# Weight-part tiles 64 bytes longer, so that the four slots of a ring start at four different offsets modulo 256 bytes

## The chip, the core and the metric

The kernel runs on one core of a Trainium2 chip. The metric is the device time of one execution in microseconds (us). TensorE (PE) multiplies, and its weight loads are listed apart as PEld; VectorE (DVE), ScalarE (ACT), GpSimd (POOL) and SyncE (SP) are the other engines. SBUF is the on-chip memory with 128 partitions; an address below is the byte within one partition, the same for all 128.

## The reference

One layer of a decoder with four parallel branches over 256 tokens of width 2048, all in float32. What matters here is that nearly all of it is products with large weight matrices, each read once:

```
xn = rms_norm(x, ln_g)
cols = jnp.split(w_in, _split_points(), axis=1)
(a_q, a_k, a_v, a_g, c_b, c_c, c_h, c_g, s_q, s_k, s_v, s_g, m_q, m_g,
 i_q, i_k, i_w, r_a, r_c, r_s, r_m) = [xn @ w for w in cols]
...
mk, mv = jnp.split(mem_n @ w_mem_kv, 2, axis=-1)
...
merged = (sigmoid(r_a) * (y_a @ w_branch[0]) + sigmoid(r_c) * (y_c @ w_branch[1])
          + sigmoid(r_s) * (y_s @ w_branch[2]) + sigmoid(r_m) * (y_m @ w_branch[3]))
return x + merged @ w_out
```

A final RMSNorm follows. The four branches are two masked attentions, an attention over 256 memory tokens and a short convolution; each is small beside the products.

## The kernel before, in words

Each float32 operand is split into a high part of type fp32r and the remainder, also fp32r, and a product is three matmuls that add into one PSUM bank: high by high, high by low, low by high. The tokens are split once and stay in SBUF: `x_hl` holds 16 chunks of 128 rows, each 256 high and 256 low values (the memory tokens lie in `m16a` and `m16b`, the gated branch results in `y`, the merged result in `mt`, all in the same form).

The weights stream. `split_weights` (L117) loads 128 partitions x 2048 values at a time on SP's queue into one of four `raw` tiles (L123), and cuts each into two halves of 1024 values. For each half `parts_tiles` (L113) takes the next slot of two rings with four slots each, `hi` and `lo`; `split` (L106) lets ACT write the high part (L107) and DVE the remainder (L108). TensorE then reads the slot. ACT can begin a slot again only when TensorE has finished with it.

There are two shapes of matmul. In `project_t` (L145, matmuls L141 to L143 in `products_t`) the weights are the stationary operand, 128 columns of 4 bytes loaded by PEld, and 256 tokens stream past; one slot serves 24 matmuls. In `project` (L166) and in `by_halves` (matmuls L162 to L164 in `products`) 128 token columns are stationary and 512 weight values stream past, except in the last two blocks of the output projection, where 256 do; one slot serves 12 matmuls in `project`. TensorE executes matmuls in the order of the program, and loads the weights of the next one beside the running one.

Addresses follow from the order and sizes of the tiles. A constant pool with a filler tile ends at byte 24,576, where `x_hl` begins, and then come `qt`, `m16b`, `m16a`, `kt` (8704 bytes, the size of its largest tenant `u`, L612), `vv`, `y`, `nat`, the four `raw`, the four `hi`, the four `lo` (4096 bytes a slot), `part`, `pt`, and a pool with `sm`, `st`, `pr` and `yt`. All sizes up to `sm` are multiples of 256 bytes, so every token tile, every slot and every `raw` tile begins at 0 modulo 256. Each row of a slot that a matmul or a weight load reads is a multiple of 512 bytes into it. Two `st` tiles take 32 bytes each, so the `pr` and `yt` tiles begin at 64 modulo 256. The last tile ends at byte 228,928 of 229,376.

Of the kernel before, what the change touches and what calls it, by code (L numbers as in the profile page):

```python
# [9 lines left out]
F32 = mybir.dt.float32  # L10
F32R = mybir.dt.float32r
# [4 lines left out]
P = 128  # L16
T = 256
# [3 lines left out]
NB = 512  # L21
# [27 lines left out]
def hybrid_kernel(ctx, tc, x, xT, mem, memT, ln_g, mem_ln_g, w_t, w_n, w_idx, conv_w, conv_b, w_mem_k, w_mem_v,  # L49
# [5 lines left out]
    big = ctx.enter_context(tc.tile_pool(name="big", bufs=1))  # L55
    rawp = ctx.enter_context(tc.tile_pool(name="rawp", bufs=4))
    spl = ctx.enter_context(tc.tile_pool(name="spl", bufs=4))
# [53 lines left out]
        return rawp.tile([P, 4 * NB], F32, name="raw", tag="raw").rearrange("p (k c) -> p k c", c=c)  # L111

    def parts_tiles(w=NB, c=NB):  # L113
        return [spl.tile([P, 2 * NB], F32R, name=n, tag=n).rearrange("p (k c) -> p k c", c=w)[:, :, :c]
                for n in ("hi", "lo")]

    def split_weights(src, w):  # L117

        c = src.shape[2]
        per, half = 4 * NB // w, 2 * NB // w  # L120
        for k0 in range(0, src.shape[1], per):
            raw = raw_tile(w)[:, :, :c]
            nc.sync.dma_start(out=raw, in_=src[:, k0:k0 + per])  # L123
            for h0 in range(0, per, half):
                hi, lo = parts_tiles(w, c)
                split(hi, lo, raw[:, h0:h0 + half])
                for k in range(half):
                    yield hi[:, k], lo[:, k], k0 + h0 + k
# [59 lines left out]
    def quarter_parts(raw):  # L188
        for h in (0, 2):
            hi, lo = parts_tiles()  # L190
            split(hi, lo, raw[:, h:h + 2])
            for i in range(2):
                yield hi[:, i], lo[:, i], h + i
# [131 lines left out]
    def to_heads(name, c0):  # L325

        dst = big.tile([P, 8, T], F32, name=name, tag=name)
        for b in range(4):
            copy_t(dst[:, 2 * b:2 * b + 2], project_t(w_t[FIRST[c0] + b], x_act))
        return dst  # L330
# [176 lines left out]
    def first_columns(dst):  # L507

        src = w_t[FIRST[M_Q]:FIRST[M_Q] + 2].rearrange("b p k c -> p k b c")
        outs = [bank("first", tag)[:, :T] for tag in "aabb"]  # L510
        xraw = big.tile([P, KC, T], F32, name="xraw", tag="m16b")
        for k0 in range(0, KC, 4):
            raw = raw_tile(NB).rearrange("p k (b c) -> p k b c", b=2)
            n = 1 if k0 == 0 else 2
            for k in range(k0, k0 + 4, n):
                nc.sync.dma_start(out=xraw[:, k:k + n], in_=xT[:, k:k + n])
                for i in range(n):
                    nc.sync.dma_start(out=raw[:, k + i - k0], in_=src[:, k + i])
                for i in range(n):
                    if (k + i) % 2 == 0:  # L520
                        hi, lo = parts_tiles(NB, NB)
                    split_tokens(xraw[:, k + i], k + i, g_x, x_hl[:, k + i])
                    h, lw = hi[:, (k + i) % 2], lo[:, (k + i) % 2]
                    split(h, lw, raw[:, k + i - k0].rearrange("p b c -> p (b c)"))
                    for j in range(4):
                        js = slice(j * P, (j + 1) * P)
                        products_t(outs[j], h[:, js], lw[:, js], k + i, KC, x_act)
        copy_t(dst[:, 0:4], outs)
# [40 lines left out]
    k = big.tile([P, 8, T], F32, name="kt", tag="kt")  # L569
# [28 lines left out]
    k = to_heads("kt", S_K)  # L598
# [6 lines left out]
    k = to_heads("kt", A_K)  # L605
# [3 lines left out]


    cc = to_heads("qt", C_C)
    u = big.tile([P, 8 * (T + 16)], F32, name="u", tag="kt")[:, :8 * (T + 2)].rearrange("p (c t) -> p c t", c=8)  # L612
    nc.gpsimd.memset(u[:, :, 0:2], 0.0)
    for b in range(4):
        acc = project_t(w_t[FIRST[C_H] + b], x_act)
# [101 lines left out]
```

## Time and profile before

| | |
|---|---|
| runs | 1414.96, 1413.65, 1413.29 us; median 1413.65 |
| profiled execution | 1414.42 us, of which the span from the first to the last instruction is 1412.6 us |
| TensorE granted clock, mean | 0.997 of full speed |
| PE busy | 1396.2 us, 99% of the span |
| PEld busy | 1263.7 us, 89% |
| DVE, ACT busy | 933.8 us (66%), 729.2 us (52%) |
| HBM | 190 GB/s over the span |

A matmul's duration counts from its start to the modelled end of its pipeline, so matmuls overlap in the records and a busy share of 99% does not say that the array runs at its peak. The distance between the starts of two successive matmuls is the time that one costs.

### The profile page before, as it was taken

The numbers are of one execution on the slowest core, as the hardware profiler recorded it, in microseconds if no ns is written. First come the engines' busy times: TensorE is split into PE (matmuls) and PEld (weight loads), VectorE is DVE, ScalarE is ACT, GpSimd is POOL, SyncE is SP. The second block draws the span as 40 slices with busy tenths as digits, with TensorE's granted clock in tenths as the row PEclk, the third lists the DMA queues.
The fourth block names the chain that finished last, engine by engine and source line by source line (L and its number), as shares of the span: only waits on it lengthen the run. The fifth ranks groups of instructions, "written<-read, shape, count | busy, mean of one in ns | idle before, by whom it ended". The sixth has DMA issues, their size and how long they took to land.

```text
span 1412.6 us, 21263 instructions
## 1 busy us (share of the span) xinstructions
PE 1396.2 (99%) x8796; PEld 1263.7 (89%) x8796; DVE 933.8 (66%) x1123; ACT 729.2 (52%) x991; POOL 11.2 (1%) x26
## 2 busy tenths in 40 slices
PE   9999999999999999999999999999999999999997
PEld 9998998789999898877999899878999999878887
DVE  7587764774747885487546876487546557788654
ACT  7663675453445585445444685445433345545443
POOL 1000000000000000000000000000000000000000
PEclk9999999999999999999999999999999999999999
DMA  9764645375553735537554645637555654736561
GB/s 342 285 243 175 208 151 179 120 268 171 178 180 120 268 125 185 198 119 254 193 180 149 238 149 185 203 120 255 193 179 180 212 182 148 267 139 244 180 202 66
DMA packets 49969, 269.49 MB, mean 191 GB/s; under 512 B 6656, under 2 KB 17456, under 8 KB 19024
## 3 DMA queue, kind: packets, MB, share of 16 engines
q1 hardware_dynamic: 48960, 264.03, 54.3%
q0 software_dynamic: 624, 3.31, 0.6%
q8 instruction: 69, 1.13, 0.3%
q10 hardware_dynamic: 288, 0.79, 0.1%
q14 instruction: 28, 0.23, 0.0%
HBM read 265.88 MB, written 2.10 MB: 190 GB/s over the span
## 4 chain that ended last, share of the span: by engine, by line
PE 87%; DVE 7%; DMA 2%; issue 2%; ACT 2%; SPq 0%; POOLq 0%; POOL 0%; DVEq 0%; ACTq 0%
PE acc L141 14%; PE acc L143 14%; PE acc L142 14%; DVE lo L108 4%; PE w L163 4%; PE w L164 4%; PE w L162 4%; PE r L162 3%; PE r L163 3%; PE r L164 3%; PE o L162 2%; PE o L163 2%; PE o L164 2%; DMA raw<-in_w_n 1%; PE y L163 1%
## 5 line engine op out<-in xcount | busy, mean ns | idle before, releaser
L108 DVE TENSOR_TENSOR lo<-raw,hi 128x1024 fp32r<-128x1024 f32 (+1 forms) x538 | 639.5, 1201 | 432.0 <-ACT hi L107 430.4
L107 ACT CAST hi<-raw 128x1024 fp32r<-128x1024 f32 (+1 forms) x538 | 551.7, 1032 | 559.1 <-PE acc L142 212.1
L142 PE MATMUL acc<-x_hl,hi 128*128 128x256 f32 x1520 | 431.2, 284 | 0.0
L143 PE MATMUL acc<-x_hl,lo 128*128 128x256 f32 x1520 | 431.0, 284 | 0.0
L141 PE MATMUL acc<-x_hl,hi 128*128 128x256 f32 x1520 | 430.5, 283 | 0.0
L142 PEld LDWEIGHTS acc<-x_hl,hi 128*128 128x128 f32 x1520 | 290.8, 191 | 0.2
L141 PEld LDWEIGHTS acc<-x_hl,hi 128*128 128x128 f32 x1520 | 290.7, 191 | 0.2
L143 PEld LDWEIGHTS acc<-x_hl,lo 128*128 128x128 f32 x1520 | 290.6, 191 | 0.1
L162 PE MATMUL w<-hi,y 128*128 128x512 f32 x256 | 99.9, 390 | 0.0
L164 PE MATMUL w<-hi,y 128*128 128x512 f32 x256 | 99.6, 389 | 0.0
L163 PE MATMUL w<-lo,y 128*128 128x512 f32 x256 | 99.6, 389 | 0.0
L162 PE MATMUL r<-hi,x_hl 128*128 128x512 f32 x248 | 96.9, 391 | 0.0
L163 PE MATMUL r<-lo,x_hl 128*128 128x512 f32 x248 | 96.6, 389 | 0.0
L164 PE MATMUL r<-hi,x_hl 128*128 128x512 f32 x248 | 96.5, 389 | 0.0
L164 PEld LDWEIGHTS w<-hi,y 128*128 128x128 f32 x256 | 48.1, 188 | 10.0
L162 PEld LDWEIGHTS w<-hi,y 128*128 128x128 f32 x256 | 48.1, 188 | 9.9
L163 PEld LDWEIGHTS w<-lo,y 128*128 128x128 f32 x256 | 48.1, 188 | 9.8
L162 PE MATMUL o<-hi,mt 128*128 128x512 f32 (+1 forms) x160 | 55.4, 347 | 0.0
L163 PE MATMUL o<-lo,mt 128*128 128x512 f32 (+1 forms) x160 | 55.3, 347 | 0.0
L162 PEld LDWEIGHTS r<-hi,x_hl 128*128 128x128 f32 x248 | 46.7, 188 | 9.6
L164 PE MATMUL o<-hi,mt 128*128 128x512 f32 (+1 forms) x160 | 55.3, 347 | 0.0
L164 PEld LDWEIGHTS r<-hi,x_hl 128*128 128x128 f32 x248 | 46.6, 188 | 9.6
(247 smaller groups left out, 1858.1 us busy)
## 6 DMA issues: line engine op xcount, KB each, us to landing
raw<-in_w_t SPq DMA_DIRECT2D x92, 1024.0 KB, 5.0
raw<-in_w_n SPq DMA_DIRECT2D x80, 1024.0 KB, 4.9
raw<-in_w_branch SPq DMA_DIRECT2D x32, 1024.0 KB, 5.2
raw<-in_w_out SPq DMA_DIRECT2D x16, 1024.0 KB, 4.8
raw<-in_w_mem_k SPq DMA_DIRECT2D x8, 1024.0 KB, 5.6
raw<-in_w_mem_v SPq DMA_DIRECT2D x8, 1024.0 KB, 5.1
raw<-in_w_t SPq DMA_DIRECT2D x16, 256.0 KB, 5.7
raw<-in_memT SPq DMA_DIRECT2D x2, 1024.0 KB, 8.0
```

What stands on the lines that cost most here:

```text
L107: nc.scalar.copy(out=hi, in_=src)
L108: nc.vector.tensor_sub(out=lo, in0=src, in1=hi.bitcast(F32))
L141: nc.tensor.matmul(o, lhsT=hi, rhs=a[:, 0], start=(k == 0), stop=False)
L142: nc.tensor.matmul(o, lhsT=hi, rhs=a[:, 1], start=False, stop=False)
L143: nc.tensor.matmul(o, lhsT=lo, rhs=a[:, 0], start=False, stop=(k == nk - 1))
L162: nc.tensor.matmul(o, lhsT=ah, rhs=hi, start=start, stop=False)
L163: nc.tensor.matmul(o, lhsT=ah, rhs=lo, start=False, stop=False)
L164: nc.tensor.matmul(o, lhsT=al, rhs=hi, start=False, stop=stop)
```

## The change

Each `hi` and `lo` tile is allocated 16 values (64 bytes) longer, and the matmuls, casts and subtractions use the first 1024 values as before. Slots of a ring now lie 4160 bytes apart, so slots 0 to 3 start at 0, 64, 128 and 192 modulo 256. A ring takes 16,640 bytes, 65 times 256, so the `lo` ring starts at 0 again and `hi` and `lo` of the same slot share their offset. To make room `u` is allocated with 8 x 264 instead of 8 x 272 values (8448 bytes, 33 times 256): the tiles from `vv` to the `hi` ring move down by 256 bytes, and those behind the `lo` ring up by 256. Their offsets modulo 256 stay. No instruction is added, removed or reshaped.

```
     def parts_tiles(w=NB, c=NB):
-        return [spl.tile([P, 2 * NB], F32R, name=n, tag=n).rearrange("p (k c) -> p k c", c=w)[:, :, :c]
+        return [spl.tile([P, 2 * NB + 16], F32R, name=n, tag=n)[:, :2 * NB].rearrange("p (k c) -> p k c", c=w)[:, :, :c]
                 for n in ("hi", "lo")]
...
-    u = big.tile([P, 8 * (T + 16)], F32, name="u", tag="kt")[:, :8 * (T + 2)].rearrange("p (c t) -> p c t", c=8)
+    u = big.tile([P, 8 * (T + 8)], F32, name="u", tag="kt")[:, :8 * (T + 2)].rearrange("p (c t) -> p c t", c=8)
```

## Rows read from the trace of the kernel before

**Rows 1.** The page: busy time of each engine (us, share of the span, instructions), TensorE's granted clock in 40 slices in tenths, and the chain that ended last, by engine and by line.

```profile
PE 1396.2 (99%) x8796; PEld 1263.7 (89%) x8796; DVE 933.8 (66%) x1123; ACT 729.2 (52%) x991; POOL 11.2 (1%) x26
...
PEclk9999999999999999999999999999999999999999
...
PE 87%; DVE 7%; DMA 2%; issue 2%; ACT 2%; SPq 0%; POOLq 0%; POOL 0%; DVEq 0%; ACTq 0%
PE acc L141 14%; PE acc L143 14%; PE acc L142 14%; DVE lo L108 4%; PE w L163 4%; PE w L164 4%; PE w L162 4%; PE r L162 3%; PE r L163 3%; PE r L164 3%; PE o L162 2%; PE o L163 2%; PE o L164 2%; DMA raw<-in_w_n 1%; PE y L163 1%
```

**Rows 2.** The whole span as one window, busy time with counts in brackets: instructions that read or write a `hi` tile, then those of a `lo` tile, then the matmuls of L141 and those of L162 alone. The last row is the group of 256-value matmuls of L162 from the groups kept apart by shape.

```profile
0.00:1412.60 1412.60, 1286.77 (x5608) 940.93 (x5608) 639.49 (x538) 551.71 (x538) 1.00 0.55 191
...
0.00:1412.60 1412.60, 903.23 (x2804) 531.69 (x2804) 639.49 (x538) 1.00 0.55 191
...
0.00:1412.60 1412.60, 482.98 (x1712) 1.00 0.55 191
...
0.00:1412.60 1412.60, 411.01 (x1092) 1.00 0.55 191
...
L162 PE MATMUL o<-hi,mt 128*128 128x256 f32 x64 | 17.9, 283 | 0.0
```

**Rows 3.** The timeline of PE from 700 to 706 us, 256 streamed columns: start in us, duration in us, instruction. First and last of 53 matmuls.

```profile
699.73 0.28 PE L142 MATMUL acc<-x_hl,hi 128*128 128x256 f32 x1
...
705.97 0.28 PE L143 MATMUL acc<-x_hl,lo 128*128 128x256 f32 x1
```

**Rows 4.** The timeline of PE from 560 to 563 us, 512 streamed columns. First and last of 15 matmuls.

```profile
559.71 0.39 PE L164 MATMUL r<-hi,x_hl 128*128 128x512 f32 x1
...
562.89 0.39 PE L163 MATMUL r<-lo,x_hl 128*128 128x512 f32 x1
```

**Rows 5.** The timeline of PE from 98.9 to 103 us, 512 streamed columns, just after a change of shape. The 0.48 us of the first matmul has a wait in it.

```profile
98.72 0.48 PE L162 MATMUL v<-hi,m16a 128*128 128x512 f32 x1
99.03 0.40 PE L163 MATMUL v<-lo,m16a 128*128 128x512 f32 x1
99.27 0.40 PE L164 MATMUL v<-hi,m16a 128*128 128x512 f32 x1
99.50 0.40 PE L162 MATMUL v<-hi,m16a 128*128 128x512 f32 x1
99.74 0.39 PE L163 MATMUL v<-lo,m16a 128*128 128x512 f32 x1
...
101.12 0.39 PE L163 MATMUL v<-lo,m16a 128*128 128x512 f32 x1
101.35 0.39 PE L164 MATMUL v<-hi,m16a 128*128 128x512 f32 x1
```

**Rows 6.** The timeline of PE from 343 to 345 us, where 68 weight columns are stationary instead of 128 and 256 tokens stream. First and last of 17 such matmuls.

```profile
343.07 0.28 PE L141 MATMUL acc<-x_hl,hi 128*68 128x256 f32 x1
...
344.94 0.28 PE L142 MATMUL acc<-x_hl,hi 128*68 128x256 f32 x1
```

**Rows 7.** Groups kept apart by shape: weight loads with 256 columns streaming beside them, and with 512 (busy us, mean ns of one, idle us before).

```profile
L141 PEld LDWEIGHTS acc<-x_hl,hi 128*128 128x128 f32 x1504 | 288.5, 192 | 0.2
...
L162 PEld LDWEIGHTS w<-hi,y 128*128 128x128 f32 x256 | 48.1, 188 | 9.9
```

**Rows 8.** The timeline of PE at 491 us and at 355 us: two passes of a plain float32 matmul, once with the streamed operand `pr` at 64 and the stationary `vv` at 0 modulo 256, once with both operands in `it` at 0.

```profile
491.91 0.39 PE L394 MATMUL yp<-pr,vv 128*128 128x128 f32 x2
...
355.45 0.39 PE L458 MATMUL lg<-it 128*128 128x128 f32 x2
```

**Rows 9.** Groups kept apart by shape on DVE and ACT: 512 values with both inputs at 0, then twice with one input at 64 and one at 0, and the cast to `y` or `hi` from 64 and from 0.

```profile
L502 DVE TENSOR_TENSOR merged<-merged,sig 128x512 f32<-128x512 f32 x24 | 15.6, 682 | 0.0
...
L344 DVE TENSOR_TENSOR yt<-yt,qt 128x512 f32<-128x512 f32 x16 | 11.0, 686 | 2.1 <-ACT qt L429 2.0
L108 DVE TENSOR_TENSOR y<-yt,y 128x512 fp32r<-128x512 f32 x16 | 10.9, 684 | 0.7 <-ACT y L107 0.7
...
L107 ACT CAST y<-yt 128x512 fp32r<-128x512 f32 x16 | 9.9, 616 | 1.5 <-DVE yt L344 1.5
...
L107 ACT CAST hi<-raw 128x512 fp32r<-128x512 f32 x16 | 9.4, 615 | 3.7 <-DMA raw<-in_w_t 3.6
```

**Rows 10.** The splits of full halves, by shape, and the waits of ACT before them (who waited for whom: us in total, times, longest).

```profile
L108 DVE TENSOR_TENSOR lo<-raw,hi 128x1024 fp32r<-128x1024 f32 x518 | 626.9, 1222 | 418.4 <-ACT hi L107 416.9
L107 ACT CAST hi<-raw 128x1024 fp32r<-128x1024 f32 x518 | 540.6, 1050 | 548.8 <-PE acc L142 205.5 <-PE w L164 95.1 <-PE r L164 71.3
...
ACT hi L107 <- PE acc L142: 212.1, 128, 2.5
...
PEld m L163 <- DVE lo L108: 5.0, 5, 1.1
```

## The prediction

> **What bounds the kernel now.** I read the page first: PE is busy for 99% of the span, the chain that ended last lies on PE for 87% and on DVE for 7%, and TensorE's granted clock is at its upper level, 2.4 GHz, in every slice [rows 1]. So the time is the number of matmuls times the distance between their starts, plus a few stretches where PE waits for a split. Next come the counts: 5608 matmuls read a `hi` tile and 2804 a `lo` tile, 8412 of 8796 together. L141 has 1712 of them, L162 has 1092 [rows 2]; each stands for three lines of equal count, so 5136 belong to `project_t` and 3276 to the other shape. Of the latter 3 x 64 = 192 stream 256 values, which makes 5328 matmuls that stream 256 columns and 3084 that stream 512.
>
> Then the distances. From 699.73 to 705.97 us there are 52 steps, 6.24 / 52 = 0.120 us each [rows 3]. From 559.71 to 562.89 there are 14 steps, 3.18 / 14 = 0.227 us [rows 4]. At 2.4 GHz 256 columns last 106.7 ns and 512 last 213.3 ns. Each matmul thus costs about 13.3 ns more than its columns, whichever shape it has. That surplus, 8412 x 13.3 ns = 112 us, is the only thing that the change can reach on TensorE. The question is whether it has to do with where the stationary and the streamed operand lie relative to each other.
>
> **What the trace says of that.** Before, every weight slot and every token tile starts at 0 modulo 256, so no row shows a weight part at another offset. Three views come near.
>
> First, the surplus isn't a constant. Just after a change of shape, the same 512-column matmul goes from 99.03 to 99.74 us in three steps, 0.237 us each, and from 99.03 to 101.35 in ten, 0.232 [rows 5]; later it settles at 0.227. With 68 stationary columns in place of 128 the 256-column matmul goes from 343.07 to 344.94 in 16 steps, 0.117 [rows 6]. And a weight load lasts 192 ns beside 256 streaming columns, 188 beside 512 [rows 7]. So the load and the stream do act on each other, and how much depends on their timing. The Trainium skill (SBUF — State Buffer, "Who interferes with whom") gives TensorE two independent read ports and says "PE and ACT never wait on anyone"; by it the change moves nothing at all, 0 us. These rows agree with it only in part: something in the pair of streams moves by up to 10 ns at one and the same offset.
>
> Second, the one matmul in which the operands differ by 64: two passes of `yp` with `pr` at 64 against `vv` at 0 take 0.39 us, and two passes of `lg` with both at 0 take 0.39 us as well [rows 8]. The distance of 64 costs nothing that shows. But this is plain float32, 128 columns at a time; it streams fewer values per ns than fp32r, so it is near evidence and no proof.
>
> Third, the other engines: a subtraction or product with one input at 64 and one at 0 takes 684 to 686 ns where both at 0 take 682, and a cast takes 616 from 64 and 615 from 0 [rows 9].
>
> **The change part by part.**
> - Longer tiles, on TensorE: three of four slots move to a new offset, so 3/4 of the matmuls are touched: 3996 of 256 columns and 2313 of 512, 6309 in all. Price unknown, bounded from both sides. From below, the whole surplus of these goes: 6309 x 13.3 ns = -84 us. From above, the surplus stays at the worst distance of the disturbed stretch, 0.237 instead of 0.227, for the 512-column shape, 2313 x 10 ns = +23 us, and, taking the same 10 ns for the other shape, 3996 x 10 = +40 us, together +63 us. The nearest row is that of the two float32 matmuls, 0.39 against 0.39, so I take 0. A step of 10 ns in two durations of two passes each leaves up to 5 ns a pass unseen there, which is why both other signs keep their chances.
> - Longer tiles, on DVE and ACT: 518 full splits of 1222 ns and 1050 ns [rows 10]. DVE's subtraction then reads `hi` at one offset and `raw` at another. By the row with unequal inputs this is +4 of 682 ns, 0.6%: 7 ns a split, 518 x 7 = 3.7 us of DVE time. It is hidden: ACT starts a split only when TensorE has freed a slot, and waits for this 212.1 us in the 256-column stages alone [rows 10]. Where it isn't hidden, DVE's 4% of the chain for L108, some 57 us, 0.6% is 0.3 us. I take 0; without the cover the whole 3.7 us would show.
> - `u` shorter, and tiles moved by 256 bytes: no offset modulo 256 changes, no instruction is reshaped, each convolution row keeps its place inside `u`. 0 us.
> - DMA: `raw` keeps its offset, sizes and order. 0 us. No wait is added, and the ring still has four slots.
>
> Sum: 1412.6 + 0 for the span. The profiled execution took 1414.42 us, 1.8 more than its span; the median of the runs is 1413.65, 0.8 below it. My forecast is the median, **1413.7 us**.
>
> **Rivals.** What a measurement of this kernel can tell from no change is about 0.2%, 2.8 us. Over 6309 matmuls that is 0.45 ns each, so if the offset matters to the surplus at all, the result will hardly look like no change.
>
> Slower: the load and the stream start within a few ns of each other, and at equal offsets they fall into the 0.227 that the 512-column shape settles at, which is the low end of what it shows. If the offset decides where they meet, slots at 64, 128 and 192 settle higher, or each new slot starts a stretch as after 99.03 us. At 0.232 this is 2313 x 5 ns = +12 us, 1425; with the whole 10 ns on this shape +23 us, 1437. It decides from 2.8 us / 2313 = 1.2 ns on. For it: the disturbed stretch, which is slower at every one of its first steps, and that a slot serves only 12 matmuls in `project`. Against: the two equal float32 pairs.
>
> Faster: the 256-column shape settles at 0.120, above the 0.117 of the 68-column loads. If equal offsets are what makes the two streams meet, the other three slots come down to 0.117, 3996 x 3 ns = -12 us, and if the 512-column shape gains as much, 2313 x 3 = -7 us: 1395. For it: the shorter load leaves the same stream faster, so part of the surplus is the load's. Against: half the columns save only 3 of 13 ns, and a load of half the length isn't another offset. The Trainium skill (TensorE: Matmul & The Clock Gate, "Back-to-back issue gap") puts the isolated warm gap at the columns over 2.4 GHz plus about 2.5 ns; by that estimate 10.8 ns of the surplus could go, 6309 x 10.8 = -68 us, 1346. No row here of an fp32r matmul comes near that gap.
>
> That the change doesn't do what it says: if the pool rounded sizes up to 256 bytes, all slots would stay at 0. The `pr` tile's 64, which two 32-byte `st` tiles make, speaks against it. It would also give 1413.7 and is part of the first case.
>
> **How the numbers follow.** No change 0.38: the only pair with unequal offsets, and the same on DVE and ACT. Slower 0.35: timing moves the surplus, and the shape with 512 columns sits at its low end. Faster 0.27: the shape with 256 columns sits above the shorter load. The likeliest case alone spans 1411 to 1416.5. For 8 in 10 the range must reach into both rivals: up to the slower one's full 10 ns on the 512-column shape, 1437, and down to the faster one's 1395, with 2 us beyond for what DVE adds or takes: 1393 to 1437. Left out are the bounds, -84 and +63 us, about one chance in ten on either side.
>
> **What would show it.** In the changed profile the starts should lie 0.120 us apart at 256 columns and 0.227 at 512 in all four slots, 24 or 12 matmuls each, weight loads should stay at 192 and 188 ns, and L108 and L107 at 1222 and 1050 ns. The forecast is wrong if the distance follows a pattern that repeats with every fourth slot. The slower rival would show as 512-column starts near 0.232 in three slots out of four while the 256-column ones stay; the faster one as 256-column starts near 0.117 and loads below 192 ns. If L108 grew by more than 1%, PE's waits for DVE's `lo`, 5.0 us before PEld's `m` now [rows 10], would grow first.

## The result: 0.5% faster, with both shapes of matmul changed, in opposite directions

The changed kernel takes 1406.61 us (median; 1406.07 to 1407.13) against 1413.51 us for the one before in the same comparison, a ratio of 0.9949 with a 95% interval of 0.9932 to 0.9966. The profiled execution took 1407.13 us with a span of 1405.4 us, 7.2 us less than the span before. The forecast was no change at 1413.7 us; its range, 1393 to 1437, holds the time.

The page of the changed kernel, first the busy times and the granted clock, then the chain that ended last by engine and by line:

```profile
PE 1389.9 (99%) x8796; PEld 1247.0 (89%) x8796; DVE 933.1 (66%) x1123; ACT 728.0 (52%) x991; POOL 11.2 (1%) x26
...
PEclk9999999999999999999999999999999999999999
...
PE 85%; DVE 9%; issue 2%; DMA 2%; ACT 2%; SPq 0%; POOLq 0%; POOL 0%; DVEq 0%; ACTq 0%
PE acc L143 13%; PE acc L141 13%; PE acc L142 13%; DVE lo L108 5%; PE w L163 4%; PE w L164 4%; PE w L162 4%; PE r L163 3%; PE r L164 3%; PE r L162 3%; PE o L163 2%; PE o L162 2%; PE o L164 2%; DMA raw<-in_w_n 1%; PE y L163 1%
```

The counts of instructions are as before, and the clock is at its upper level in every slice again [rows 1]; its mean is 0.999 of full speed against 0.997. That is not the gain: executions of the kernel before that ran at 0.999 took 1412.9 to 1413.8 us. So it is the same matmuls, at the same level of the clock, closer together. Each engine's instructions also come in the same order as before.

Where it comes from stands in the timeline, if one knows where the slots change. A ring deals its slots out in the order 0, 192, 128, 64 (bytes modulo 256, by the addresses in the built program), and project_t uses one for 24 matmuls. These are PE's rows at which a new slot begins, from the timeline at 690 to 705 us (start, duration, instruction); the offsets are, in order, 0, 192, 128, 64, 0 and 192:

```profile
690.70 0.28 PE L141 MATMUL acc<-x_hl,hi 128*128 128x256 f32 x1
...
693.58 0.28 PE L141 MATMUL acc<-x_hl,hi 128*128 128x256 f32 x1
...
696.30 0.28 PE L141 MATMUL acc<-x_hl,hi 128*128 128x256 f32 x1
...
699.14 0.28 PE L141 MATMUL acc<-x_hl,hi 128*128 128x256 f32 x1
...
701.88 0.28 PE L141 MATMUL acc<-x_hl,hi 128*128 128x256 f32 x1
...
704.76 0.28 PE L141 MATMUL acc<-x_hl,hi 128*128 128x256 f32 x1
```

Divided by 24: 2.88 us is 0.120 a matmul in the slot at 0, 2.72 is 0.113 at 192, 2.84 is 0.118 at 128, 2.74 is 0.114 at 64, and 2.88 is 0.120 again at 0. Before, all were at 0.120 [rows 3].

The same for 512 streamed columns, 12 matmuls a slot, at 562 to 577 us, offsets 0, 192, 128, 64, 0:

```profile
562.31 0.39 PE L162 MATMUL r<-hi,x_hl 128*128 128x512 f32 x1
...
565.06 0.39 PE L162 MATMUL r<-hi,x_hl 128*128 128x512 f32 x1
...
567.86 0.39 PE L162 MATMUL r<-hi,x_hl 128*128 128x512 f32 x1
...
570.65 0.39 PE L162 MATMUL r<-hi,x_hl 128*128 128x512 f32 x1
...
573.40 0.39 PE L162 MATMUL r<-hi,x_hl 128*128 128x512 f32 x1
...
576.14 0.39 PE L162 MATMUL r<-hi,x_hl 128*128 128x512 f32 x1
```

Here 2.75 is 0.229 at 0, 2.80 is 0.233 at 192, 2.79 is 0.2325 at 128, 2.75 is 0.229 at 64, and 2.74 is 0.228 at 0 again. Before it was 0.227 [rows 4]. Even the slot at 0 is slower, because each change of slot disturbs it: over all slots at 0 in `project` the first five steps average 231.7 ns and the last six 226.9, so the 12 matmuls of a slot are just enough to settle, as behind a change of shape before [rows 5].

Over the whole trace, from all start times, with steps over 135 or 260 ns set apart as waits and changes of shape (a step counts for the slot whose weights are loaded in it at 256 columns, and streamed in it at 512):

```
mean ns between starts, fp32r          before    after: slot at 0     64    128    192
256 columns streamed, weights stationary 119.9            119.5  114.8  118.5  114.4
512 weight columns streamed              227.1            229.5  229.7  232.4  233.2
```

Over all slots the steps at 256 columns average 116.8 ns in place of 119.9, which is -16.5 us for some 5330 of them; those at 512 columns average 231.2 in place of 227.2, +12.5 us for 3084; and what the steps set apart take beyond a usual step falls from 20.9 to 17.4 us, -3.5 us. Together -7.5 us, against 7.2 in the span. The last term goes with the longer 512-column matmuls: in the two runs below that change one shape's slots alone it is 16.0 us where those are longer, and 19.8 where they are not. That the next split gains time beside a longer matmul is the likely reason.

DVE and ACT did as forecast. Groups of the changed kernel kept apart by shape (busy us, mean ns, idle us and what ended it), with the weight loads of both shapes:

```profile
L108 DVE TENSOR_TENSOR lo<-raw,hi 128x1024 fp32r<-128x1024 f32 x518 | 627.3, 1224 | 414.4 <-ACT hi L107 413.2
L107 ACT CAST hi<-raw 128x1024 fp32r<-128x1024 f32 x518 | 539.7, 1048 | 548.3 <-PE acc L142 195.0 <-PE w L164 98.3 <-PE r L164 74.2
...
L141 PEld LDWEIGHTS acc<-x_hl,hi 128*128 128x128 f32 x1504 | 284.4, 189 | 0.3
...
L162 PEld LDWEIGHTS w<-hi,y 128*128 128x128 f32 x256 | 48.1, 188 | 11.1
```

1222 became 1224 ns and 1050 became 1048 [rows 10]; the loads beside 256 columns fell from 192 to 189 ns, those beside 512 stayed at 188 [rows 7].

### The profile page after: what moved, and what is told of

Same layout as the page of the kernel before. It is cut to its first block, busy times and chain, and to the rows that moved or that the text cites. A ratio compares the mean times of both kernels' runs of the same rounds, so it can differ in the third digit from the quotient of the medians.

```text
span 1405.4 us, 21264 instructions
## 1 busy us (share of the span) xinstructions
PE 1389.9 (99%) x8796; PEld 1247.0 (89%) x8796; DVE 933.1 (66%) x1123; ACT 728.0 (52%) x991; POOL 11.2 (1%) x26
## 4 chain that ended last, share of the span: by engine, by line
PE 85%; DVE 9%; issue 2%; DMA 2%; ACT 2%; SPq 0%; POOLq 0%; POOL 0%; DVEq 0%; ACTq 0%
PE acc L143 13%; PE acc L141 13%; PE acc L142 13%; DVE lo L108 5%; PE w L163 4%; PE w L164 4%; PE w L162 4%; PE r L163 3%; PE r L164 3%; PE r L162 3%; PE o L163 2%; PE o L162 2%; PE o L164 2%; DMA raw<-in_w_n 1%; PE y L163 1%
## 5 line engine op out<-in xcount | busy, mean ns | idle before, releaser
L142 PE MATMUL acc<-x_hl,hi 128*128 128x256 f32 x1520 | 426.5, 281 | 0.0
L143 PE MATMUL acc<-x_hl,lo 128*128 128x256 f32 x1520 | 425.9, 280 | 0.0
L141 PE MATMUL acc<-x_hl,hi 128*128 128x256 f32 x1520 | 425.3, 280 | 0.0
L141 PEld LDWEIGHTS acc<-x_hl,hi 128*128 128x128 f32 x1520 | 286.6, 189 | 0.3
L143 PEld LDWEIGHTS acc<-x_hl,lo 128*128 128x128 f32 x1520 | 286.4, 189 | 0.1
L142 PEld LDWEIGHTS acc<-x_hl,hi 128*128 128x128 f32 x1520 | 286.1, 188 | 0.3
L162 PE MATMUL w<-hi,y 128*128 128x512 f32 x256 | 100.6, 393 | 0.0
L162 PE MATMUL r<-hi,x_hl 128*128 128x512 f32 x248 | 97.4, 393 | 0.0
L162 PEld LDWEIGHTS w<-hi,y 128*128 128x128 f32 x256 | 48.1, 188 | 11.1
L162 PEld LDWEIGHTS r<-hi,x_hl 128*128 128x128 f32 x248 | 46.6, 188 | 10.5
L163 PEld LDWEIGHTS r<-lo,x_hl 128*128 128x128 f32 x248 | 46.5, 188 | 10.5
L164 PE MATMUL o<-hi,mt 128*128 128x512 f32 (+1 forms) x160 | 55.5, 348 | 0.0
```

Source lines behind the costliest of these rows:

```text
L141: nc.tensor.matmul(o, lhsT=hi, rhs=a[:, 0], start=(k == 0), stop=False)
L142: nc.tensor.matmul(o, lhsT=hi, rhs=a[:, 1], start=False, stop=False)
L143: nc.tensor.matmul(o, lhsT=lo, rhs=a[:, 0], start=False, stop=(k == nk - 1))
L162: nc.tensor.matmul(o, lhsT=ah, rhs=hi, start=start, stop=False)
L163: nc.tensor.matmul(o, lhsT=ah, rhs=lo, start=False, stop=False)
L164: nc.tensor.matmul(o, lhsT=al, rhs=hi, start=False, stop=stop)
```

## The experiments

**Theory A**: the offset, modulo 256 bytes, between where the stationary operand of the next matmul and the streamed operand of the running one start decides how much they cost each other. **Rivals**: what helps is that the four slots differ from each other (B); the address of the weights by itself (C); the tiles that move along with the slots, on DVE and ACT (D); the move by 256 bytes (F).

### All slots at one offset: 64, 128, 192

`u` fixes where everything behind it lies. Its size alone is changed; the rings keep 4096-byte slots, all alike:

```
-    u = big.tile([P, 8 * (T + 16)], F32, name="u", tag="kt")...
+    u = big.tile([P, 8 * (T + 2) + 0], F32, name="u", tag="kt")...     # 64;  + 16: 128;  + 32: 192
```

> All slots of both rings, raw, vv, y, part and pr lie 64 bytes further from the tokens (u is allocated with 8 x 258 values), so the weights are at 64 modulo 256 to x_hl, m16a, m16b, x_sums and mt, and at 0 to y; the four slots of a ring are all alike. Theory A, the offset between the stationary and the streamed operand sets the distance of starts: 256 columns at 0.114 us as the changed kernel's slot at 64 shows (median), 5136 x -6 ns = -31 us; 512 columns 0.230 instead of 0.227 except for the 768 that read y, 2316 x 3 ns = +7; together about 1390 us. Rival B, what helps is that the four slots differ from each other, so that ACT and DVE write one while TensorE reads another: all slots are alike here, so 1413.5 us and 0.120.

Measured: 1397.88 us, 0.9895 (0.9878 to 0.9911). B is out: the slots are alike, and the gain is over twice that of the change. But A had asked for 1390. The steps of the 256-column shape averaged 0.1161, not 0.114, the 512-column shape 0.2299 and, against `y`, 0.2269. The timeline shows why it fell short. These are two stretches of PE in the run with 64, at 390 to 396 us and at 700 to 706 us, first and last rows:

```profile
389.81 0.28 PE L142 MATMUL acc<-x_hl,hi 128*128 128x256 f32 x1
...
395.93 0.28 PE L142 MATMUL acc<-x_hl,hi 128*128 128x256 f32 x1
...
699.73 0.28 PE L142 MATMUL acc<-x_hl,hi 128*128 128x256 f32 x1
...
705.97 0.28 PE L141 MATMUL acc<-x_hl,hi 128*128 128x256 f32 x1
```

54 steps in 6.12 us are 0.1133; 53 steps in 6.24 us are 0.1177. Same instruction, same offset, two distances, and each keeps itself up: one stage of 1536 matmuls, from 986.8 us on, stays at 0.118 from its first to its last, another of 672, from 356.2 us on, stays at 0.113 once its first few steps are past. Which one it is was set at the start of the stretch or by a wait within it. All five stages that follow directly on the 512-column shape began at 0.118, and the one at 0.113 began behind a step of 0.31 us.

> As with 64, but everything behind u lies 128 bytes further. Theory A from the changed kernel's slot at 128: 256 columns at 0.119, 5136 x -1 ns = -5 us; 512 columns at 0.232, 2316 x 5 ns = +12; about 1420 us, slower than before. Rival B: 1413.5 us.

Measured: 1419.44 us, 1.0042 (1.0027 to 1.0057): slower, as A said, with 0.1194 and, against all but `y`, 0.2325.

> As with 64, but 192 bytes further. Theory A from the changed kernel's slot at 192: 256 columns at 0.113, 5136 x -7 ns = -36 us; 512 columns at 0.233, 2316 x 6 ns = +14; about 1391 us. Rival B: 1413.5 us.

Measured: 1410.84 us, 0.9981 (0.9971 to 0.9990). A was 20 us too hopeful: 256 columns averaged 0.1176 and nearly all steps were 0.117 to 0.119, where the changed kernel's slot at 192 had 0.1144. So A as it stood can't tell the distance from the offset alone. That it is relative is plain in one place of this run, though. `y` and the slots moved together, `x_hl` did not. Groups by shape, first four of the kernel before, then three of this run:

```profile
L142 PE MATMUL acc<-x_hl,hi 128*128 128x256 f32 x1504 | 426.8, 284 | 0.0
...
L141 PE MATMUL acc<-x_hl,hi 128*128 128x256 f32 x1504 | 426.0, 283 | 0.0
...
L162 PE MATMUL w<-hi,y 128*128 128x512 f32 x256 | 99.9, 390 | 0.0
...
L162 PE MATMUL r<-hi,x_hl 128*128 128x512 f32 x248 | 96.9, 391 | 0.0
```

```profile
L142 PE MATMUL acc<-x_hl,hi 128*128 128x256 f32 x1504 | 420.8, 280 | 0.0
...
L162 PE MATMUL w<-hi,y 128*128 128x512 f32 x256 | 99.9, 390 | 0.0
L162 PE MATMUL r<-hi,x_hl 128*128 128x512 f32 x248 | 97.9, 395 | 0.0
```

The matmuls that read `y` last 390 ns as before, those of the same shape that read `x_hl` went from 391 to 395. From start to start it is plainer: with the slots at 64, 128 and 192 the steps against `y` stay at 227 ns, and the others are at 229.9, 232.5 and 233.3.

### Everything moved together, and the move by 256 bytes alone

```
-    fill = const.tile([P, 56], F32, name="fill")
+    fill = const.tile([P, 40], F32, name="fill")
```

> The filler tile is 64 bytes shorter, so tokens, slots and all other large tiles move together to 192 modulo 256 and keep their offsets to each other at 0. Theory A, the offset between the operands decides: 1413.5 us, 0.120 and 0.227. Rival C, the address of the weights itself modulo 256 decides: as the changed kernel's slot at 192, 0.113 and 0.233, about 1391 us.

Measured: 1413.62 us, 1.0001 (0.9992 to 1.0010), with 0.1199 and 0.2271. C is out. The interval also says what "no change" looks like here: 0.1% either way.

```
-    u = big.tile([P, 8 * (T + 16)], F32, name="u", tag="kt")...
+    u = big.tile([P, 8 * (T + 8)], F32, name="u", tag="kt")...
```

> The change's second line alone: u with 8 x 264 values, slots as before. vv, y, raw and the rings lie 256 bytes lower, nothing changes modulo 256. Theory A: 1413.5 us, 0.120 and 0.227. Rival F, the move by 256 bytes brings the gain of the change: 1406.6 us.

Measured: 1413.97 us, 1.0001 (0.9992 to 1.0010). F is out; the second line of the change only makes room.

### An offset for each shape

With the `score` tile in `y`'s space there is room for slots of 4352 bytes, 17 times 256. Each use of a slot can then begin at a byte of its own:

```
-        return [spl.tile([P, 2 * NB], F32R, name=n, tag=n)...
+        at = 16 if w == TB else 0
+        return [spl.tile([P, 2 * NB + 64], F32R, name=n, tag=n)[:, at:at + 2 * NB]...
...
-        score = const.tile([P, 384], F32, name="score")
+        score = big.tile([P, 384], F32, name="score", tag="y")
```

> Slots are 4352 bytes long, all at 0 modulo 256; where the weights are cut in pieces of 256 columns a slot is used from byte 64 on, else from byte 0 (the score tile lies in y's space to make room, u as in the change). So the 256-column shape of project_t sees 64 and the 512-column shape sees 0. Theory A: 4944 matmuls at the 0.1161 us that the run with 64 showed on average instead of 0.1199, -19 us, and 512 columns at 0.227 throughout: about 1394.5 us; down to 1382 if most stages settle at the 0.1135 that half of them showed there, up to 1403 if most settle at 0.1178. Rival D, the gain of the run with 64 came from the tiles that moved with the slots (raw, vv, y, part): these are back at 0, so 1413.5 us.

Measured: 1398.09 us, 0.9892 (0.9876 to 0.9909). D is out: `raw`, `vv`, `y` and `part` are back at 0 and the gain is still there. The 512-column shape is back at 0.2271; the 256-column shape got 0.1167, since more of its stages settled at the longer distance than in the run with 64.

Now the change itself, one shape at a time (the start is at 0, 192, 128, 64 bytes in turn for one shape, at 0 for the other). The edit goes by the width of the weight pieces, so two small stages of 192 matmuls each go with the other shape than their own: the first projection, which cuts its weights in pieces of 512 columns, and the last two blocks of the output projection, which have pieces of 256.

```
+    ring = itertools.cycle((0, 48, 32, 16))
...
+        at = next(ring)
+        at = at if w == TB else 0          # the other run: if w != TB
```

> Slots of 4352 bytes, all at 0 modulo 256; pieces of 256 columns start at 0, 192, 128, 64 bytes in turn, as the changed kernel's slots do, pieces of 512 columns always at 0. The change's first half by shape. If its gain is project_t's alone: 256 columns at 0.1168 on average instead of 0.1199, 5136 x -3.1 ns = -16 us, 512 columns at 0.227: 1397.5 us. If the two shapes' slots act on each other or the waits fill up: not far from 1406.6.

Measured: 1397.86 us, 0.9889 (0.9873 to 0.9906), with 119.6, 114.9, 118.6 and 114.3 ns at 0, 64, 128 and 192, and 227.1 for the other shape.

> The other half: pieces of 512 columns start at 0, 192, 128, 64 in turn, pieces of 256 columns at 0. 512 columns at 0.2312 instead of 0.2271, 3084 x 4.1 ns = +13 us, less some 4 us of waits for splits that longer matmuls cover: 1422 us, 0.120 at 256 columns. If the 512-column shape loses nothing by itself: 1413.5.

Measured: 1422.31 us, 1.0061 (1.0046 to 1.0076), with 229.6, 229.6, 232.3 and 233.2 ns at 0, 64, 128 and 192, and 119.9 for the other shape. The two halves, -15.5 and +9.0 us against the kernel before, add up to -6.5; the change measured -6.9. Groups by shape of the second run (its L145 and L166 are L141 and L162 before), to be held against the 283, 390 and 391 ns of the same groups before, shown above:

```profile
L145 PE MATMUL acc<-x_hl,hi 128*128 128x256 f32 x1504 | 426.0, 283 | 0.0
...
L166 PE MATMUL w<-hi,y 128*128 128x512 f32 x256 | 100.6, 393 | 0.0
...
L166 PE MATMUL r<-hi,x_hl 128*128 128x512 f32 x248 | 97.4, 393 | 0.0
```

### Other offsets

```
+    leads = itertools.cycle([4 * n for n in (0, 4, 8, 12, 1, 5, 9, 13, 2, 6, 10, 14, 3, 7, 11, 15)])
...
+        at = lead["now"] if w == TB else 0        # lead["now"] = next(leads) at each call of project_t
```

> Same tiles, but each call of project_t uses its slots from another byte on: 0, 64, 128, 192, 16, 80, 144, 208, 32, 96, 160, 224, 48, 112, 176, 240, and again. The time says little; the distance of starts of 256-column matmuls by offset does. Theory A with a pattern that repeats every 128 bytes: about 0.120 at 0 and 128, 0.1135 or 0.1175 at 64 and 192, and equal values at offsets 128 apart. Rival E, only the distance modulo 64 or the line that the first byte lies in counts: offsets 16, 32 and 48 as 0.

One run, 1406.78 us. Rows of PE at which a call of 96 matmuls begins, at offsets 32, 96, 160, 224 and 48:

```profile
672.49 0.28 PE L145 MATMUL acc<-x_hl,hi 128*128 128x256 f32 x1
...
683.84 0.28 PE L145 MATMUL acc<-x_hl,hi 128*128 128x256 f32 x1
...
695.11 0.28 PE L145 MATMUL acc<-x_hl,hi 128*128 128x256 f32 x1
...
706.63 0.28 PE L145 MATMUL acc<-x_hl,hi 128*128 128x256 f32 x1
...
717.83 0.28 PE L145 MATMUL acc<-x_hl,hi 128*128 128x256 f32 x1
```

11.35, 11.27, 11.52 and 11.20 us over 96 are 0.118, 0.117, 0.120 and 0.117. Over the run the means were 119.9 ns at 0, 118.3 at 16, 118.2 at 32, 117.8 at 48, 117.7 at 64 and 117.8 at 192, 118.7 at 128, and 116.7 to 120.0 at the rest. E is out: 16, 32 and 48 are not as 0. A pattern of 128 bytes holds for 64 and 192, but 32 and 160 (118.2 and 120.0) and 80 and 208 (118.8 and 116.7) differ, so it is not shown either. As an offset can have more than one distance, one pass over the offsets can't settle it. Entered from 0 with a whole call between changes, 64 settled at the longer distance, and so did 192, entered here from 128.

### Choosing the shorter distance

In the changed kernel a slot at 192 always follows one at 0, and it was at 0.113 from the first matmuls on. If the step sets the distance and the distance keeps itself up, an occasional slot at 0 is enough:

```
+        if next(calls) % 1 == 0:                  # the other run: % 4, in project_t
+            lead.append(0)
...
+        at = lead.pop() if w == TB and lead else 48 if w == TB else 0
```

> Pieces of 256 columns start at 192, except the first slot of each call of project_t, which starts at 0 (24 of its 96 matmuls); 512 columns at 0. Theory A2: at 64 or 192 two spacings keep themselves up, 0.1135 and 0.118, and which one depends on how load and stream meet at the start; a step from 0 to 192 gave the short one every time in the changed kernel. Then 3708 x -6.2 ns = -23 us: about 1390.5 us. Rival G, no such state, 192 means the 0.1176 that the run with 192 had and the changed kernel's 0.1135 comes from something else: 3708 x -2.3 = -9: 1405 us.

Measured: 1392.32 us, 0.9850 (0.9835 to 0.9864), with 0.1142 at 192.

> As the one before, but only every fourth call of project_t begins with a slot at 0. Theory A2, if the state lasts until the next disturbance: 4632 x -6.2 ns = -29 us, 1385 us, and up to 1392 if the matmuls of the attention between them end it early. Rival G: 4632 x -2.3 = -11: 1403 us.

Measured: 1388.38 us, 0.9821 (0.9806 to 0.9835), the fastest of all, and 1.3% below the changed kernel. G is out for both. 3400 of 4547 steps at 192 were 113 or 114 ns, where the run with all slots at 192 had 193 of 5050 there and 4243 at 117 or 118. The timeline of this run, where a slot at 0 begins, where 192 begins, and where the next slot at 0 begins:

```profile
665.67 0.28 PE L145 MATMUL acc<-x_hl,hi 128*128 128x256 f32 x1
...
668.54 0.28 PE L145 MATMUL acc<-x_hl,hi 128*128 128x256 f32 x1
...
709.34 0.28 PE L145 MATMUL acc<-x_hl,hi 128*128 128x256 f32 x1
```

24 matmuls at 0 in 2.87 us are 0.120, and the 15 slots after them, 360 matmuls in 40.80 us, are 0.1133 to the end.

Where the short distance was lost, a wait or another shape had come between. Behind a step of 0.31 us at 356.8 us of this run the slots at 192 stayed at the longer one for three calls, and the next slot at 0 brought the short one back. Rows at which a call begins, the second of them with a slot at 0:

```profile
368.33 0.28 PE L145 MATMUL acc<-x_hl,hi 128*128 128x256 f32 x1
...
390.94 0.28 PE L145 MATMUL acc<-x_hl,hi 128*128 128x256 f32 x1
...
401.98 0.28 PE L145 MATMUL acc<-x_hl,hi 128*128 128x256 f32 x1
...
412.86 0.28 PE L145 MATMUL acc<-x_hl,hi 128*128 128x256 f32 x1
```

192 matmuls in 22.61 us are 0.118; after the call with the slot at 0, 96 in 10.88 us are 0.113.

The direction of the step fits all runs with these offsets: down by 64 (0 to 192, 128 to 64) gave about 0.114 in the changed kernel and here, up by 64 (0 to 64, 128 to 192) gave 0.118 in all six calls of the run with other offsets that had no wait in them. No run varies the direction alone.

### The wide shape

```
+        if w != TB:
+            at = 4 * (0, 4, 8, 12, 1, 5, 9, 13, 2, 6, 10, 14, 3, 7, 11, 15)[next(wide) // 8 % 16]
```

> Project_t's slots as in the last one (192, every fourth call begins at 0); pieces of 512 columns start at another byte every eight slots: 0, 64, 128, 192, 16, 80, 144, 208, 32, 96, 160, 224, 48, 112, 176, 240. Asked: does the 512-column shape have an offset better than 0? By theory A and the run with this shape's slots in turn: 0.227 at 0 once it has settled, 0.230 at 64, 0.232 at 128, 0.233 at 192, the others between 0.227 and 0.236, none below 0.226. If one is at 0.224 or less, 3084 x -3 ns = -9 us is left to be had.

One run, 1399.93 us. At 0 the distance was 227.0 ns, at 64 229.4, at 128 232.4, at 192 233.3, and at the twelve others 230.1 to 234.6. None is below that of 0: there was nothing left to be had for this shape among them.

## Why the prediction was wrong, by its own steps

- **What bounds the kernel, and the 13.3 ns surplus as all that the change can reach**: right in the main. Clock, counts, DVE and ACT stayed, and the distances of starts moved. One term was left out: the waits, which the prediction held unchanged, fell by 3.5 us, half of the net gain.
- **The price on TensorE, taken as 0**: this is the step that failed. It rested on two plain float32 matmuls, 0.39 us each at offsets of 64 and 0 [rows 8]. The fp32r matmuls do depend on the offset: 119.9 ns at 0, 113 to 118 at 64 and 192, 119 at 128; and 227, 230, 233 and 232 ns at 0, 64, 192 and 128. In place of 0 the two shapes moved by -16.5 and +12.5 us. The row was near in kind but not in rate: a plain float32 pass takes 109 to 114 ns from start to start for 128 columns, an fp32r matmul 120 ns for 256. Whether that is why it showed nothing, no run tells. The text had the better row in its hands: fp32r matmuls whose distance moved by 10 ns at a single offset [rows 5], which is a sign that the two streams act on each other.
- **The rivals**: what each expected of one shape happened, and both happened at once. The slower one's price was 0.232 in three slots and +12 us for the 512-column shape; measured 0.2318 there, and +12.5 with the slot at 0, which that price left out. The faster one's was 0.117 in three slots and -12 us for the 256-column shape; measured 0.1159 on average, 0.114 to 0.115 in two slots and 0.1185 in the third, and -16.5 us. The fault was to give them separate chances, as if one offset had one sign for the kernel. Nor did the 512-column shape gain in the faster rival's manner.
- **The number**: that the time came out only 7 us from the forecast is luck. Two changes of over 12 us nearly cancel; either half alone lies 9 or 15 us from the kernel before.
- **The slot at 0 inside a changing ring**: the slower rival had it that each new slot starts a disturbed stretch. It does for 512 columns: the slots at 0 went from 227 to 229.5.
- **DVE and ACT, 0 us**: right within 2 ns a split. **`u` and DMA, 0 us**: right, 1.0001 with the second line alone.
- **The signs to look for**: "a pattern that repeats with every fourth slot" is what the timeline shows.
- **The page on SBUF**: the Trainium skill (SBUF — State Buffer, "Who interferes with whom") has TensorE's two read ports independent. In the run with 64, where DVE's and ACT's splits last 1222 and 1050 ns as before, the steps of `project_t` average 0.1161 us in place of 0.1199 with both operands at one offset. So the two streams of one engine do act on each other, and the measurement decides. What inside the memory or the engine makes it so, no run here shows.

What stays open: why a step down by 64 goes with the shorter of the two distances and a step up with the longer, while starts behind a wait set now one and now the other; and whether a third, still shorter one exists. The shortest that any run held was 0.113, 6.6 ns above the 106.7 ns of 256 columns.

## What to carry to other kernels

When PE is bound and its matmuls are spaced evenly at more than their columns at the granted clock, look at the surplus per matmul, not at the busy share, and try where the stationary and the streamed tile start relative to each other; the same offset can help one shape and hurt another, so set it by shape. A change that rotates through offsets measures all of them in one trace, in the order in which it meets them: split the starts by slot before you read the total. And when a mean lies between two values, plot the steps: here 0.116 was a mixture of 0.113 and 0.118, each lasting for a whole stage, and a slot in sixteen was enough to choose.

## What the runs showed of the hardware that was not expected

- An fp32r matmul with a fresh weight load each time costs here 13 to 14 ns, some 32 cycles of 2.4 GHz, above its columns when both operands start at the same offset modulo 256: 119.9 and 227.1 ns for 256 and 512 columns. Moving both together by 64 bytes changes nothing (1413.62 us), nor does a move of the weights by 256 bytes against the tokens (1413.97 us).
- Weights that start 64 or 192 bytes further than the tokens, modulo 256, make 256-column matmuls faster (113 to 118 ns) and 512-column matmuls slower (229.9 and 233.3 ns).
- At one offset there can be two distances that keep themselves up, 0.1133 and 0.1177 over stretches of hundreds of matmuls. Which one holds is set at the start, by a wait, or by a step from another offset; a slot at 0 before those at 192 chose the shorter one and brought the kernel to 1388.38 us.
